# A hybrid encoder layer on one core: fewer idle matmuls, a recurrence prepared a step later, and a reordered final norm

## The chip, the core and the metric

The kernel runs on one NeuronCore of a Trainium2 chip. Its engines work side by side, each through a queue of its own: TensorE (PE, matrix products, with its weight loads shown apart as PEld), VectorE (DVE), ScalarE (ACT), GpSimd (POOL), and SyncE (SP), which issues most transfers between the chip's main memory and the core's own memory. The metric is the time of one execution on the device in microseconds (us); the median of three runs is 2256.15 us.

## The reference

One encoder layer over two groups of 256 tokens with 2048 features; both groups use the same weights.

```python
def encoder_layer(h, ...):
    xn = rmsnorm(h, norm_mix_w)
    proj = xn @ w_in                                  # 2048 x 7200
    y_na = neighbourhood_attention(q, k, v, na_rpb)   # 8 heads of 128, on a grid 4 x 64
    y_dn = gated_deltanet_bidir(qkv, z, b, a, ...)    # 8 heads of 128, chunks of 64 tokens
    h = h + concatenate([y_na, y_dn]) @ w_out
    hn = rmsnorm(h, norm_ffn_w)
    return h + (silu(hn @ w_gate) * (hn @ w_up)) @ w_down     # 5632 wide
# afterwards: rmsnorm(h, final_norm_w)
```

The gated delta rule passes a state of 128 x 128 per head from chunk to chunk, forward over the tokens and, in a second copy, backward. In each chunk:

```python
v_new = u_i - w_i @ S
o = (q_i * exp(g_i)) @ S + qk_i @ v_new
S = S * exp(g_last) + (k_i * exp(g_last - g_i)).T @ v_new
```

The output of both directions is added, normalised per head, and gated by silu(z). The final norm multiplies each token by 1 / sqrt(mean of squares + eps) and each feature by its weight.

## The kernel before

**Layout.** Features lie on the 128 partitions, the 512 tokens of both groups along the row: a tile of 128 features x 512 tokens is one of 16 row tiles of h. Large products are made in fp32r with operands split into a high and a low part, three matmuls for each (`mm3`: high x high, high x low, low x high). `load_w` loads a weight block through SP and splits it: `w_hi` on ACT (L138), `w_lo` on DVE (L139). Half of a column tile (`half_gemm`) is 8 x 3 matmuls of 128 x 512.

**Start.** While the first weights and rows of x arrive, `WARM` = 36 matmuls of 128 x 256 on a tile of ones in bf16 keep TensorE running; their result is not used. `load_first` splits weights (L274, L275) and `split_x` splits x (`xhi` on ACT, L256, `xlo` on DVE, L257). The first two column tiles then go row tile by row tile: six matmuls for each.

**The order of the work.** All matmuls and transposes are pinned to the order in which the program writes them. Small work is woven into the large products by generators: after every six large matmuls `half_gemm` calls `pump`, which advances the first generator of the queue `chains` and then the first of `side`. One such call is a step; `yield from pause(n)` lets n steps pass. The other engines' queues are ordered by the planner of the framework, by the order in the program and its own cost estimates; `tc.high_priority` moves the weight splits ahead.

**The recurrence.** Heads go in pairs. For a pair, two column tiles give v (each evacuated by `evac`, tile `ev_xi`, convolved on DVE in `conv_silu`, tile `cacc`, and passed through silu on ACT into `dvT`, L361), then `start_waiting` appends `prepare` of both heads, joined by `together`, to `side`, and `recur_pair` to `chains`. `prepare(h)` waits until the pair before has run its recurrence, fetches `uq` (POOL) and `kq` (SP) where that hasn't been done, pauses `2 + h % 2` steps, and transposes vT and kq in four blocks each (L90); ACT copies the first into `dvn` (L778), DVE scales the second into `kd` (L783). `recur_pair` waits for both heads, pauses `CORE_START` = 2 steps and runs four chunk steps. In each, `ps_s<-S,kq`, then DVE's `r` (L814), then `ps_s<-r,uq` and ACT's `n` (L828), then `ps_s<-n,kd` and the new state `S` (L848), with fixed pauses of 3, 2 and 2 steps between. At its end `finish_pair` goes to `side`: ACT takes eight squares (`yo`, L876), one step later DVE makes the factors (`ssq`, Newton steps L162 to L167, L882) and scales the outputs `os` (L887), and after `FIN_GAP` = 5 more steps TensorE transposes them (`ps_s<-ident,os`). The two z tiles of the pair follow the v tiles; after the last pair, the products of w_out with the attention half cover what is left of the recurrence.

**The end.** `finish` adds the last segment of w_down to h for one half of the tokens after the other (`hT`, L1318), squares each row tile (`f_sq`, L1355), scales it by the norm weight (L1356) and sums the squares (L1358). The last row tile's squares aren't summed there: `final_norm` sums `acc` and the last `sq` over the partitions with matmuls against ones, into one PSUM column for each 128 tokens, takes root and reciprocal (`sd`), scales the identity by each (`dgs`, L1334, two instructions on DVE), and one matmul of ones with `dgs` spreads the factors over all partitions. DVE multiplies h in six pieces (L1343), and SP stores each piece. The first half's norm runs within the second half's products; the second half's is the end of the program. PSUM tiles of the small work come from `sm_tile` (three banks).

Of the kernel before, what the change touches and what calls it, by code (L numbers as in the profile page):

```python
# [12 lines left out]
AF = mybir.ActivationFunctionType  # L13
ALU = mybir.AluOpType
# [4 lines left out]
P = 128  # L19
# [40 lines left out]
OPEN_AT = 0  # L60
HALF, BAND = 32, 40

WARM = 36

ROW_FACTORS = 24
DECAY_HEAD = 3
# [3 lines left out]
def r32(ap):  # L70
    return ap.bitcast(F32)
# [3 lines left out]
def hybrid_encoder(ctx: ExitStack, tc: tile.TileContext, xT, w_in, w_ba, w_out, w_gate,  # L75
# [3 lines left out]
    act = nc.scalar.activation  # L79
    tt = nc.vector.tensor_tensor  # L80
    ts = nc.vector.tensor_scalar
# [4 lines left out]
    def mm(*a, **k):  # L86
        pin(nc.tensor.matmul(*a, **k))  # L87

    def transpose(*a):
        pin(nc.tensor.transpose(*a))  # L90
# [12 lines left out]
    ones = cons.tile([P, P], F32, name="ones")  # L103
# [3 lines left out]
    ident = cons.tile([P, P], F32, name="ident")  # L107
# [92 lines left out]
    def pause(n):  # L200
        for _ in range(n):
            yield
# [11 lines left out]
    def col_tile(src, xs):  # L214
        ps = pg.tile([P, T], F32, tag="g", name="ps_g")
        half_gemm(ps, src[0], xs[:8], True, False)
        half_gemm(ps, src[1], xs[8:], False, True)
        return ps
# [20 lines left out]
    def sm_tile():  # L239
        return psm.tile([P, T], F32, tag="s", name="ps_s")  # L240
# [19 lines left out]
    ps = sm_tile()  # L260
    idle = ones.bitcast(BF16)
    for _ in range(WARM):
        mm(ps[:, :2 * P], idle[:, :P], idle, start=True, stop=True)
# [349 lines left out]
    for h in range(H):  # L613
        kq = wk.tile([P, 2, T], F32, tag="kq", bufs=2, name="kq")
        ps = (ps_k0, ps_k1)[h] if h < 2 else col_tile(w_in[2 * h], xs)
        conv_silu(ps, 8 + h, kq[:, 0])
        ps = (ps_q0, ps_q1)[h] if h < 2 else col_tile(w_in[2 * h + 1], xs)
        conv_silu(ps, h, kq[:, 1])
        sq = na.tile([P, T], F32, tag="qT", name="q_sq")
# [27 lines left out]
    ps = sm_tile()  # L647
# [66 lines left out]
    for h in range(H):  # L714
        ps = col_tile(w_in[16 + 3 * h], xs)
# [4 lines left out]
        ps = col_tile(w_in[16 + 3 * h + 1], xs)  # L720
# [4 lines left out]
        ps = col_tile(w_in[16 + 3 * h + 2], xs)  # L725
# [26 lines left out]
    def fetch(h):  # L752

        uq = state["UQ"][2 * (h % 2):2 * (h % 2) + 2]
        kq = wk.tile([P, 2, T], F32, tag="kq", bufs=2, name="kq2")
        nc.sync.dma_start(kq, s_kq[h])
        for b in range(NB):
            for hf in range(2):
                nc.gpsimd.dma_start(
                    uq[b][half[hf], :, :, hf * C:hf * C + C].rearrange("s i w c -> s (i w) c"),  # L760
                    s_uq[h * NB + b, hf].rearrange("s i w c -> s (i w) c"))
        fetched[h] = uq, kq

    def prepare(h, vT):

        dr = state["dr"]
        while h > 1 and not {h - 2, h - 2 ^ 1} <= traced:
            yield
        if h not in fetched:
            fetch(h)  # L770
        uq, kq = fetched[h]
        yield from pause(2 + h % 2)
        pv, pk = sm_tile(), sm_tile()
        for t, u in ((pv, vT), (pk, kq[:, 0])):
            for i in range(4):
                transpose(t[:, i * P:i * P + P], u[:, i * P:i * P + P], ident)
        vn = na.tile([P, NB, 2, P], F32, tag=("vT", "s1")[h % 2], name="dvn")
        nc.scalar.copy(vn, pv.rearrange("p (b q d) -> p b q d", b=NB, q=2))  # L778
        kd = dr.tile([P, 3, NB, P], F32, tag="kd", bufs=2, name="kd")
        pk4 = pk.rearrange("p (b q d) -> p b q d", b=NB, q=2)  # L780
        for st in range(3):
            pp = 0 if st in (0, 3) else 1
            tt(kd[:, st], pk4[:, :, pp],  # L783
               scs[:, st, h * NB:h * NB + NB, None].broadcast_to([P, NB, P]), ALU.mult)
        prepared[h] = (uq, kq, vn, kd)
        yield
# [121 lines left out]
    def start_waiting():  # L908
        open_recurrence()
        while state and waiting:  # L910
            h, vT = waiting.pop(0)
            side.append(together(prepare(h, vT[0]), prepare(h + 1, vT[1])))
            chains.append(recur_pair(h))

    late = []
    for h in range(0, H, 2):
        vT = []
        for i in range(2):
# [9 lines left out]
            ps = pg.tile([P, T], F32, tag="g", name="ps_g")  # L928
# [10 lines left out]
        for i in range(h, h + 2):  # L939
            ps = col_tile(w_in[40 + 2 * i + 1], xs)  # L940
# [24 lines left out]
    for i in pairs:  # L965
        ps = pg.tile([P, T], F32, tag="g", name="ps_g")
# [9 lines left out]
    for i in pairs[:2]:  # L976
        ps = pg.tile([P, T], F32, tag="g", name="ps_g")
# [20 lines left out]
    acc = gA.tile([P, T], F32, tag="acc", name="ssq_acc2")  # L998
    A11, S3, S1, A12, S2, S4, A22 = range(7)
    for n, i in enumerate(pairs):  # L1000
# [3 lines left out]
        else:  # L1004
            hk = st.tile([P, T], F32, tag="hk", bufs=2, name="hk")
            nc.sync.dma_start(hk, s_h1[i])
            ps = pg.tile([P, T], F32, tag="g", name="ps_g")
# [19 lines left out]
        sq = acc if n == 0 else st.tile([P, T], F32, tag="sq", name="h_sq")  # L1027
# [163 lines left out]
    for p in range(NPAIR):  # L1191
# [8 lines left out]
        if p // 2 == FIRST_SEG:  # L1200
            k = p % 2 * 2
# [31 lines left out]
    def ring(shape, nm):  # L1233
        return fq.tile([P] + shape, F32, tag="ra", bufs=5, name=nm)
# [86 lines left out]
    def final_norm(b, acc, sq):  # L1321
        t0, t1 = b * L, b * L + L
        yield from pause(2)
        ps = sm_tile()
        for i in range(2):
            for part in (acc, sq):
                mm(ps[:, i:i + 1], part[:, i * P:i * P + P], ones[:, :1], start=(part is acc),
                   stop=(part is sq), skip_group_check=True)
        sd = cons.tile([P, 2], F32, tag="sd", bufs=2, name="sd3")
        act(out=sd, in_=ps[:, :2], func=AF.Sqrt, scale=1.0 / D, bias=epsc)  # L1330
        nc.vector.reciprocal(sd, sd)
        dgs = qp.tile([P, 2, P], F32, tag="dgs", name="dgs")
        for i in range(2):
            ts(dgs[:, i], ident, sd[:, i:i + 1], None, ALU.mult)  # L1334
        yield from pause(3 if b == 0 else 0)
        rs = sm_tile()[:, :L]
        mm(rs, ones, dgs.rearrange("p i t -> p (i t)"), start=True, stop=True)
        if b:
            out = r32(state["new_sA"]()).rearrange("p a k t -> p (a k t)") \
                .rearrange("p (k t) -> p k t", t=L)  # L1340
        for k, n in ((0, 2), (2, 2), (4, 4), (8, 4), (12, 2), (14, 2)):
            yo = out[:, k:k + n] if b else ring([n, L], "yo")
            tt(yo, hT[k // 8][:, k % 8:k % 8 + n, t0:t1],  # L1343
               rs[:, None, :].broadcast_to([P, n, L]), ALU.mult)
            nc.sync.dma_start(y[b, k // 4, :, k % 4:k % 4 + n], yo)
            yield

    def finish(s, aseg, b, keep):

        t0, t1 = b * L, b * L + L  # L1350
        acc = qp.tile([P, L], F32, tag="acc", bufs=2, name="ssq_acc3")
        for n in down_half(s, aseg, t0, t1, keep):
            hk = hrow(n)[:, t0:t1]
            sq = acc if n == 0 else qp.tile([P, L], F32, tag="fsq", bufs=2, name="f_sq")
            act(out=sq, in_=hk, func=AF.Square)  # L1355
            act(out=hk, in_=hk, func=AF.Copy, scale=nwl[:, n:n + 1])  # L1356
            if 0 < n < 15:
                tt(acc, acc, sq, ALU.add)  # L1358
            pump()
        chains.append(final_norm(b, acc, sq))  # L1360
# [98 lines left out]
```

## Time and profile before

| | |
|---|---|
| median of 3 runs | 2256.15 us (2255.93 to 2256.17) |
| profiled execution | 2255.7 us, its span 2253.9 us |
| busy: PE, PEld, DVE, ACT, POOL | 2239.9, 1919.7, 1776.7, 1031.2, 236.6 us |
| share of the chain that ended last | PE 95%, DVE 2%, DMA 1%, ACT 1%, issue 1% |
| transfers | 381.20 MB, mean 169 GB/s |

In timeline rows the first column is the start in us from the span's start, the second the time from the first to the last of the row's instructions, then engine, line, operation, out<-in, shape and count; the brackets give the idle time of the engine before them and what ended it. Rows of waits give who waited, for whom, and us in total, times, longest. Rows of windows give, for a stretch, its length and the busy us (and count) of PE, PEld, DVE, ACT and POOL, then TensorE's granted clock, the mean busy share of the 16 DMA engines, and GB/s. The ends of matmuls are modelled: two that follow each other overlap in the trace, and only their starts tell how fast they go.

### The profile page before, as it was taken

Reading aid. Unit: us, or ns where it says so; the run is one execution under the profiler, and the core shown is the slowest. Engines: PE = TensorE matmul, PEld = TensorE weight load, DVE = VectorE, ACT = ScalarE, POOL = GpSimd, SP = SyncE. Lnnn points to the kernel's source line nnn. Section 1 sums busy time; section 2 is a strip of 40 time slices with the busy share of each in tenths; the row PEclk is TensorE's granted clock in tenths of the full one; section 3 lists DMA queues with packets and bytes.
Section 4 is the critical chain, followed back from the end, with each engine's and each line's share of the span. In section 5 each row is a group of like instructions: output and inputs, shape, how many; then the busy total and the mean of one; then the engine's idle time right before and its main releaser. Section 6 shows DMA issues by size and latency. Waiting matters only on the chain.

```text
span 2253.9 us, 32472 instructions
## 1 busy us (share of the span) xinstructions
PE 2239.9 (99%) x12314; PEld 1919.7 (85%) x12314; DVE 1776.7 (79%) x2728; ACT 1031.2 (46%) x1548; POOL 236.6 (10%) x370
## 2 busy tenths in 40 slices
PE   9999999999999999999999999999999999999998
PEld 7888888888888888888888888888888888888887
DVE  7954799964566537888888888888888798898966
ACT  6664433333443325554444444444444464444435
POOL 1321000010000011101101111101100001001010
PEclk9999999999999999999999999999999999999999
DMA  5344322363333555777777777777777467667682
GB/s 210 130 140 148 108 97 94 106 147 122 105 104 103 192 177 187 210 203 202 203 207 199 194 199 203 215 204 202 201 195 195 147 177 212 175 179 205 175 206 84
DMA packets 112540, 381.20 MB, mean 169 GB/s; under 512 B 14048, under 2 KB 14384, under 8 KB 112128
## 3 DMA queue, kind: packets, MB, share of 16 engines
q1 hardware_dynamic: 77552, 266.25, 34.9%
q0 software_dynamic: 33680, 110.78, 23.7%
q8 instruction: 97, 1.59, 0.3%
q10 hardware_dynamic: 1152, 2.10, 0.3%
q14 instruction: 59, 0.48, 0.1%
HBM read 343.66 MB, written 35.41 MB: 168 GB/s over the span
## 4 chain that ended last, share of the span: by engine, by line
PE 95%; DVE 2%; DMA 1%; ACT 1%; issue 1%; DVEq 0%; ACTq 0%
PE ps_g L87 36%; PE ps_c L87 14%; PE ps_d L87 14%; PE ps_a L87 14%; PE ps_s L87 8%; PE ps_b L87 7%; DMA w_raw<-in_w_in_dram 1%; PE ps_s L90 1%; PE ps_o L87 1%; DVE w_lo L139 1%; DVE cacc L357 0%; PE ps_e L87 0%; ACT yo L876 0%; ACT w_hi L138 0%; DVE aA L1343 0%
## 5 line engine op out<-in xcount | busy, mean ns | idle before, releaser
L87 PE MATMUL ps_g<-xhi,w_hi 128*128 128x512 f32 x880 | 351.4, 399 | 0.0
L87 PE MATMUL ps_g<-xhi,w_lo 128*128 128x512 f32 x880 | 343.4, 390 | 0.0
L87 PE MATMUL ps_g<-xlo,w_hi 128*128 128x512 f32 x880 | 342.8, 390 | 0.0
L138 ACT ACTIVATE w_hi<-w_raw 128x1024 fp32r<-128x1024 f32 x164 | 173.3, 1058 | 270.5 <-PE ps_g L87 209.6
L138 ACT ACTIVATE w_hi<-b 128x1024 fp32r<-128x1024 f32 (+1 forms) x180 | 185.8, 1032 | 238.0 <-issue 119.4
L139 DVE TENSOR_TENSOR w_lo<-w_raw,w_hi 128x1024 fp32r<-128x1024 f32 x164 | 200.3, 1221 | 100.3 <-ACT w_hi L138 100.0
L138 ACT ACTIVATE w_hi<-w_first 128x1024 fp32r<-128x1024 f32 (+1 forms) x180 | 185.5, 1030 | 180.9 <-PE ps_c L87 90.8
L139 DVE TENSOR_TENSOR w_lo<-w_first,w_hi 128x1024 fp32r<-128x1024 f32 (+1 forms) x180 | 213.8, 1188 | 60.2 <-ACT w_hi L138 56.7
L139 DVE TENSOR_TENSOR w_lo<-b,w_hi 128x1024 fp32r<-128x1024 f32 (+1 forms) x180 | 213.0, 1184 | 7.2 <-ACT w_hi L138 6.7
L87 PEld LDWEIGHTS ps_g<-xhi,w_lo 128*128 128x128 f32 x880 | 165.2, 188 | 36.1 <-DVE w_lo L139 0.4
L87 PEld LDWEIGHTS ps_g<-xhi,w_hi 128*128 128x128 f32 x880 | 165.4, 188 | 35.6 <-issue 2.9
L87 PEld LDWEIGHTS ps_g<-xlo,w_hi 128*128 128x128 f32 x880 | 165.5, 188 | 32.4
L87 PE MATMUL ps_d<-xc,w_hi 128*128 128x512 f32 x704 | 175.1, 391 | 0.0
L87 PE MATMUL ps_c<-xc,w_hi 128*128 128x512 f32 x704 | 175.1, 391 | 0.0
L87 PE MATMUL ps_a<-xc,w_hi 128*128 128x512 f32 x696 | 173.1, 391 | 0.0
L87 PEld LDWEIGHTS ps_c<-xc,w_hi 128*128 128x128 f32 x704 | 129.4, 188 | 25.0
L87 PEld LDWEIGHTS ps_d<-xc,w_hi 128*128 128x128 f32 x704 | 129.3, 188 | 25.0
L87 PEld LDWEIGHTS ps_a<-xc,w_hi 128*128 128x128 f32 x696 | 127.9, 188 | 24.8
L138 ACT ACTIVATE w_hi<-w_second 128x1024 fp32r<-128x1024 f32 (+1 forms) x60 | 62.0, 1033 | 93.2 <-DVE ga L1153 50.3
L87 PE MATMUL ps_d<-xc,w_lo 128*128 128x256 f32 x704 | 98.5, 283 | 0.0
L87 PE MATMUL ps_c<-xc,w_lo 128*128 128x256 f32 x704 | 98.5, 283 | 0.0
L87 PE MATMUL ps_a<-xc,w_lo 128*128 128x256 f32 x696 | 97.4, 283 | 0.0
(389 smaller groups left out, 4211.7 us busy)
## 6 DMA issues: line engine op xcount, KB each, us to landing
w_raw<-in_w_in_dram SPq DMA_DIRECT2D x108, 512.0 KB, 3.3
b<-in_w_gate_dram SPq DMA_DIRECT2D x66, 512.0 KB, 4.2
b<-in_w_up_dram SPq DMA_DIRECT2D x66, 512.0 KB, 4.6
b<-in_w_group_dram SPq DMA_DIRECT2D x48, 448.0 KB, 4.2
w_raw<-in_w_out_dram SPq DMA_DIRECT2D x32, 512.0 KB, 3.5
w_raw<-in_w_down_dram SPq DMA_DIRECT2D x24, 512.0 KB, 3.6
w_second<-in_w_gate_dram SPq DMA_DIRECT2D x22, 512.0 KB, 7.0
w_first<-in_w_gate_dram SPq DMA_DIRECT2D x22, 512.0 KB, 4.3
```

What stands on the lines that cost most here:

```text
L87: pin(nc.tensor.matmul(*a, **k))
L90: pin(nc.tensor.transpose(*a))
L138: act(out=hi, in_=src, func=AF.Copy)
L139: tt(lo, src, r32(hi), ALU.subtract)
```

## The change

There are five edits. `WARM` goes from 36 to 30. `prepare` pauses `3 + h % 2` steps rather than `2 + h % 2`. In `final_norm`, both matmuls on `acc` come ahead of both on the last squares, and only the first of the four has the start flag; the scaling of the identity for the second 128 tokens goes to ACT; and the first two output pieces have one and three row tiles rather than two and two.

```diff
--- before.py
+++ after.py
@@ -60,7 +60,7 @@
 OPEN_AT = 0
 HALF, BAND = 32, 40
 
-WARM = 36
+WARM = 30
 
 ROW_FACTORS = 24
 DECAY_HEAD = 3
@@ -769,7 +769,7 @@
         if h not in fetched:
             fetch(h)
         uq, kq = fetched[h]
-        yield from pause(2 + h % 2)
+        yield from pause(3 + h % 2)
         pv, pk = sm_tile(), sm_tile()
         for t, u in ((pv, vT), (pk, kq[:, 0])):
             for i in range(4):
@@ -1322,23 +1322,23 @@
         t0, t1 = b * L, b * L + L
         yield from pause(2)
         ps = sm_tile()
-        for i in range(2):
-            for part in (acc, sq):
-                mm(ps[:, i:i + 1], part[:, i * P:i * P + P], ones[:, :1], start=(part is acc),
+        for part in (acc, sq):
+            for i in range(2):
+                mm(ps[:, i:i + 1], part[:, i * P:i * P + P], ones[:, :1], start=(part is acc and i == 0),
                    stop=(part is sq), skip_group_check=True)
         sd = cons.tile([P, 2], F32, tag="sd", bufs=2, name="sd3")
         act(out=sd, in_=ps[:, :2], func=AF.Sqrt, scale=1.0 / D, bias=epsc)
         nc.vector.reciprocal(sd, sd)
         dgs = qp.tile([P, 2, P], F32, tag="dgs", name="dgs")
-        for i in range(2):
-            ts(dgs[:, i], ident, sd[:, i:i + 1], None, ALU.mult)
+        act(out=dgs[:, 1], in_=ident, func=AF.Copy, scale=sd[:, 1:2])
+        ts(dgs[:, 0], ident, sd[:, 0:1], None, ALU.mult)
         yield from pause(3 if b == 0 else 0)
         rs = sm_tile()[:, :L]
         mm(rs, ones, dgs.rearrange("p i t -> p (i t)"), start=True, stop=True)
         if b:
             out = r32(state["new_sA"]()).rearrange("p a k t -> p (a k t)") \
                 .rearrange("p (k t) -> p k t", t=L)
-        for k, n in ((0, 2), (2, 2), (4, 4), (8, 4), (12, 2), (14, 2)):
+        for k, n in ((0, 1), (1, 3), (4, 4), (8, 4), (12, 2), (14, 2)):
             yo = out[:, k:k + n] if b else ring([n, L], "yo")
             tt(yo, hT[k // 8][:, k % 8:k % 8 + n, t0:t1],
                rs[:, None, :].broadcast_to([P, n, L]), ALU.mult)
```

## The prediction

> **What bounds the kernel now.** I read the page first (engines, chain, groups), then TensorE's waits, then the timeline at the three places that the diff touches: the start, the recurrence, the end.
>
> ```profile
> span 2253.9 us, 32472 instructions
> PE 2239.9 (99%) x12314; PEld 1919.7 (85%) x12314; DVE 1776.7 (79%) x2728; ACT 1031.2 (46%) x1548; POOL 236.6 (10%) x370
> ```
>
> TensorE is busy 2239.9 of 2253.9 us: all that a change outside the matmuls can win is in the other 14 us, and in gaps between matmuls that the modelled ends hide. The profiled execution took 2255.7 us (1.8 around its span); the median of the runs is 2256.15, so 0.45 is added at the end. TensorE's own waits (what waited <- for what: us, times, longest):
>
> ```profile
> PE ps_s L90 <- ACT dvT L361: 1.5, 3, 0.6
> ...
> PE ps_s L87 <- DVE epsc L110: 1.1, 1, 1.1
> ...
> PE ps_s L90 <- DVE os L887: 0.3, 1, 0.3
> ```
>
> The first row is `prepare`, which the diff moves by one step; the last is `finish_pair`, which follows from it. TensorE's order is the order written in the program, so a time won at any place reaches the end, unless a later operand was ready only just in time. I found no such place after the start: these waits are nearly all.
>
> **Six fewer idle matmuls.** The start in the timeline:
>
> ```profile
> 1.25 2.13 PE L87 MATMUL ps_s<-ones 128*128 128x256 bf16 x9
> 2.74 1.49 PE L87 MATMUL ps_s<-ones 128*128 128x256 bf16 x6
> 6.76 1.15 PE L87 MATMUL ps_s<-ones 128*128 128x256 bf16 x9
> 7.42 0.49 PE L87 MATMUL ps_s<-ones 128*128 128x256 bf16 x3
> 7.67 0.48 PE L87 MATMUL ps_g<-xhi,w_hi 128*128 128x512 f32 x1
> ...
> 6.31 0.75 DVE L257 SCALAR_TENSOR_TENSOR xlo<-x_raw,nwm,xhi 128x512 fp32r<-128x512 f32 x1 [0.74 <-ACT xhi L256]
> ...
> 9.44 1.42 DVE L257 SCALAR_TENSOR_TENSOR xlo<-x_raw,nwm,xhi 128x512 fp32r<-128x512 f32 x2 [0.77 <-ACT xhi L256]
> ...
> 10.73 0.39 PE L87 MATMUL ps_g<-xlo,w_hi 128*128 128x512 f32 x1
> ...
> 2.00:3.00 1.00, 1.00 (x7) 0.69 (x6) 0.00 (x0) 0.22 (x2) 0.92 (x4) 1.00 0.53 122
> ```
>
> Nine idle matmuls take 2.13 us and six 1.49: one each (2.13 - 1.49)/3 = 0.213 us. Late, nine take 1.15 and three 0.49: 0.110 each. So the rate doubles at about 6.7 (the granted clock, 1.00 in the last row, doesn't show it), when some 27 of the 36 have run; the six that go are fast ones, 6 x 0.110 = 0.66 us, and the first real matmul could start at 7.0. Its operands are there: xhi released the xlo split at 6.31, which ends at 7.06, in time for the second matmul. Next to be late is xlo of the third row tile: the two splits from 9.44 are 0.71 each, so the first is done at 10.15 to 10.2, and the matmul that reads it starts at 10.73, a margin of 0.54. The start thus gains at least 0.54 less some 0.05 of signalling: **0.49**, bounds 0 (a transfer that comes later in another execution takes the margin) and 0.66.
>
> The Trainium skill (TensorE: Matmul & The Clock Gate, part 1) says that the array runs at half clock for its first 3.4 us or so of activity, whatever the number of matmuls, and that the window runs freely. By it the step were at 1.06 + 3.4 = 4.5, the 36 would end near 6.7 and the 30 near 6.0, xhi would come last, and this part would gain some 0.35. The trace disagrees: the step is at 6.7, 5.6 us in. By its other half the step may come later than the thirtieth matmul in some executions; then real matmuls do the warming that idle ones did, which costs nothing against before.
>
> **The recurrence prepared one step later.** A step is one `pump`, six matmuls. `prepare` transposes vT and kq of a pair's two heads in two successive steps; the second head's vT comes late. Without and with a wait (second pair):
>
> ```profile
> 86.28 10.89 PE ps_g L87 x48
> ...
> 591.44 0.39 PE L87 MATMUL ps_g<-xhi,w_lo 128*128 128x512 f32 x1
> 591.67 0.60 PE L90 MATMUL ps_s<-ident,dvT 128*128 128x128 f32 x4
> ...
> 592.46 0.47 PE L87 MATMUL ps_g<-xhi,w_hi 128*128 128x512 f32 x1
> ...
> 593.70 0.40 PE L87 MATMUL ps_g<-xhi,w_lo 128*128 128x512 f32 x1
> 594.67 0.85 PE L90 MATMUL ps_s<-ident,dvT 128*128 128x128 f32 x4 [0.58 <-ACT dvT L361]
> ...
> 595.72 0.48 PE L87 MATMUL ps_g<-xhi,w_hi 128*128 128x512 f32 x1
> ```
>
> A step is 6 x 10.89/48 = 1.36 us. From matmul to matmul the round takes 592.46 - 591.44 = 1.02 without and 595.72 - 593.70 = 2.02 with the wait: 1.00, though only 0.58 shows as idle, so 0.42 more each. Three waits of 1.5 in all cost 1.5 + 3 x 0.42 = **2.8 us**. One step (1.36) is more than the longest wait (1.00), so by itself the edit ends all three. The transfers, vn and kd of `prepare`, and the first core step, move with it: recurrence steps stay as far apart as they were, and the last pair ends long before the w_out products that cover it.
>
> What follows is in the queue `side`, which runs one generator at a time. Steps are counted by the 128x512 matmuls in the timeline, from the z tile of head 0 (its first is 12); between 587.76 and 591.67, steps 47 and 49, lie twelve. Pair 0 ends its recurrence at step 41, `finish_pair` transposes at 47, and only then `prepare` of the second pair runs (49, 50; its v tiles ended at 43). So the second pair is late by two steps, not one (51, 52); the third by three (81, 82 for 78, 79, since it waits for the second pair to be traced). The third now ends at 108, after the last v tile (107), so `prepare` of the fourth goes ahead of the third's `finish_pair`: 111, 112 for 113, 114, two steps earlier, yet free of the finishing work that held up its conv on DVE. The refill of uq (POOL) and kq (SP) starts when the earlier pair is done and has seven steps to its first use, where the third pair had six without a wait of TensorE.
>
> `finish_pair` is next to be late. Its squares (ACT), factor chain and scaling (DVE) end just before its transposes:
>
> ```profile
> 582.98 0.38 DVE L880 TENSOR_SCALAR ssq<-ssq 128x8 f32<-128x8 f32 x1 [2.81 <-ACT yo L876]
> ...
> 586.86 1.43 DVE L887 TENSOR_TENSOR os<-os,ssq 128x256 f32<-128x256 f32 x4
> 588.21 0.68 DVE L307 TENSOR_TENSOR ev_xi<-ps_g,rstd 128x512 f32<-128x512 f32 x1
> 589.14 1.22 DVE L139 TENSOR_TENSOR w_lo<-w_raw,w_hi 128x1024 fp32r<-128x1024 f32 x1
> ...
> 582.86 1.04 ACT L138 ACTIVATE w_hi<-w_raw 128x1024 fp32r<-128x1024 f32 x1
> ...
> 587.76 1.30 PE L90 MATMUL ps_s<-ident,os 128*128 128x128 f32 x8
> ...
> 667.58 1.03 PE L90 MATMUL ps_s<-ident,os 128*128 128x128 f32 x8
> ...
> 717.24 1.30 PE L90 MATMUL ps_s<-ident,os 128*128 128x128 f32 x8
> ...
> 787.15 1.30 PE L90 MATMUL ps_s<-ident,os 128*128 128x128 f32 x8 [0.29 <-DVE os L887]
> ```
>
> Eight take 1.03 where nothing is late and 1.30 where the scaling ends beside them. In pair 0 the eight squares now straddle the weight split that ACT makes after step 43 (1.04); the DVE split (1.22) then falls into DVE's wait rather than into the chain, so I count 0.5 more wait there, and 0.2 left at the second pair's vT, whose ev_xi stands behind this chain. The third pair's finish gets a `prepare` ahead of it as the second's had (1.03): 0.3 won. The fourth's I leave. So 2.8 - 0.5 - 0.2 + 0.3 = **2.4**. Bounds: below, 2.8 + 0.3 less a wait of 1.04 + 1.22 = 2.3 at pairs 0 and 3: -1.5; above, all finish waits gone too (three rounds of 1.30 - 1.03 and the idle 0.29): 2.8 + 1.1 = 3.9. I take the middle, since the queued order on DVE is the planner's and unknown.
>
> **The end.** The square sums change their order and a start flag, the two scalings split over DVE and ACT, the pieces their sizes:
>
> ```profile
> 2242.52 0.38 PE L87 MATMUL ps_s<-ones,f_sq 128*128 128x1 f32 x2 [0.59 <-ACT f_sq L1355]
> ...
> 2242.98 0.36 PE L87 MATMUL ps_s<-ones,f_sq 128*128 128x1 f32 x2
> 2243.38 0.26 ACT L1330 ACTIVATE sd<-ps_s,epsc 128x2 f32<-128x2 f32 x1 [0.38 <-PE ps_s L87]
> 2243.68 0.17 DVE L1331 RECIPROCAL sd<-sd 128x2 f32<-128x2 f32 x1 [1.66 <-ACT sd L1330]
> 2243.88 0.48 DVE L1334 TENSOR_SCALAR dgs<-ident,sd 128x128 f32<-128x128 f32 x2
> ...
> 2245.21 4.74 DVE L1343 TENSOR_TENSOR aA<-hT,ps_s 128x512 f32<-128x512 f32 x6 [0.85 <-PE ps_s L87]
> ...
> 779.49 0.40 ACT L876 ACTIVATE yo<-os,rqs 128x128 f32<-128x128 f32 x1
> ...
> 2248.00:2249.00 1.00, 0.00 (x0) 0.00 (x0) 1.00 (x2) 0.00 (x0) 0.00 (x0) 0.50 0.70 274
> ...
> 2250.00:2251.00 1.00, 0.00 (x0) 0.00 (x0) 0.00 (x0) 0.00 (x0) 0.00 (x0) 0.50 1.05 414
> ```
>
> Square sums first: behind the late f_sq now stand three pairs, 0.46/2 = 0.23 apart; then two. **0.23** won. Scalings on two engines: 0.48 on DVE against one ACT scaling; nearest row, 128x128 with a scale per partition, 0.40: **0.08** won, bounds -0.1 (signalling to a further engine) and 0.2. It waits for DVE's reciprocal; behind it in ACT's queue stands nothing at the end, and the next f_sq and hT scaling in the first half, where TensorE has a full row of matmuls before it needs them. First piece of one row: the pieces (1, 3) hold the rows of (2, 2), so the third piece, and all behind it, leave DVE at the same time; the DMA engines (share 0.70 in the slice where they wait for it, then 1.05) are busy from there on. A first piece earlier by half of a 0.68 piece fills no later gap: **0**, bounds 0 and 0.3. The same edits for the first half of the tokens lie under the matmuls of the second; uncovered they would be worth the same 0.3.
>
> **Sum**: 0.49 + 2.4 + 0.3 = 3.2. Span 2253.9 - 3.2 = 2250.7, execution 2252.5, median 2253.0.
>
> **Rivals.** *The waits only change place*: the finish chain, or ev_xi behind it on DVE, takes what dvT gave back. For it: ev_xi begins right behind os at 588.21. Against: the fourth pair escapes it. Gain 0.8: 2255.3.
>
> *Slower*: the two weight splits both land in the finish chain of pairs 0 and 3, which wait 2.3 more each. The transposes stand in TensorE's fixed order and all matmuls wait behind them. 0.49 + 2.8 + 0.3 - 4.6 = -1.0: 2257.2; it decides from 1.8 us per finish on. For it: DVE sat idle 2.81 us before the chain rather than doing ev_xi. The Trainium skill (TensorE: Matmul & The Clock Gate, part 1, engine queue depths) calls the DVE queue strictly in order, and this row agrees. Against: today's chain holds one of the splits at 0.3.
>
> *More*: finish waits go too and the start gives 0.66: 0.66 + 3.9 + 0.5 = 5.1, 2251.1. *The start doesn't pay*, its margin taken by a late transfer: 2253.5.
>
> **How the numbers follow.** Forecast 0.66 (own range 2251.8 to 2254.2), waits change place 0.12, start doesn't pay 0.08, more 0.08, slower 0.06. Range 2251.0 to 2255.4 leaves out the slower rival and edges of the others. 0.2% is 4.5 us, about what a measurement of this kernel can tell from no change: only "more" gets there, in part: faster 0.07; slower by that much needs three finish waits of the rival's size: 0.03; the same 0.90.
>
> **What would show it.** First real matmul near 7.0, and ps_g split margins near zero at the third row tile; no row dvT among TensorE's waits; prepare at steps 15, 16, 51, 52, 81, 82, 111, 112; sd some 0.23 after the first f_sq pair less than now. Wrong if the os row grows beyond 2 us, or if a new wait for r or S appears.

## The result, and the profile after

The changed kernel takes 2253.36 us (median; 2251.93 to 2254.94), the kernel before, measured beside it, 2256.27 (2254.84 to 2257.85): a ratio of 0.9986, 95% interval 0.998 to 0.9992, so 2.9 us less. The forecast was 2253.0. The profiled execution of after took 2253.6 us with a span of 2251.8; its counterpart of before had 2255.7 and 2253.9.

The page of after, its first lines, TensorE's share of the chain that ended last, and the group of matmuls that read w_lo:

```profile
span 2251.8 us, 32459 instructions
...
PE 2238.1 (99%) x12308; PEld 1918.6 (85%) x12308; DVE 1776.8 (79%) x2726; ACT 1031.3 (46%) x1550; POOL 236.6 (11%) x370
...
PE 91%; DVE 4%; DMA 2%; issue 1%; ACT 1%; POOL 0%; SPq 0%; DVEq 0%; ACTq 0%; POOLq 0%
...
L87 PE MATMUL ps_g<-xhi,w_lo 128*128 128x512 f32 x880 | 343.4, 390 | 0.8 <-DVE w_lo L139 0.8
```

The chain was 95% TensorE before and is 91% now: DVE and DMA have come into it. TensorE's waits of after say where (who waited <- for whom: us in total, times, longest):

```profile
PE ps_g L87 <- DVE w_lo L139: 0.8, 1, 0.8
PE ps_s L90 <- ACT dvn L778: 0.7, 2, 0.4
PE ps_g L87 <- DVE xlo L257: 0.6, 2, 0.3
```

The waits for dvT (1.5, three times) and for os are gone. New are a wait for w_lo, which the prediction did not have at all, two short ones for dvn, and two for xlo at the start.

**The start** of after, in the timeline:

```profile
6.39 0.51 PE L87 MATMUL ps_g<-xhi,w_hi 128*128 128x512 f32 x1
7.18 0.50 PE L87 MATMUL ps_g<-xlo,w_hi 128*128 128x512 f32 x1 [0.28 <-DVE xlo L257]
...
10.87 0.50 PE L87 MATMUL ps_g<-xlo,w_hi 128*128 128x512 f32 x1 [0.29 <-DVE xlo L257]
...
10.06 1.42 DVE L257 SCALAR_TENSOR_TENSOR xlo<-x_raw,nwm,xhi 128x512 fp32r<-128x512 f32 x2 [1.29 <-ACT xhi L256]
```

The first product matmul is 1.28 us earlier than before (7.67). The fourteenth, the first that reads xlo of the third row tile, is not: 10.87 against 10.73. The split that makes this xlo starts at 10.06 against 9.44.

**At 320 us** the w_lo wait; after, then before:

```profile
319.40 0.40 PE L87 MATMUL ps_g<-xlo,w_hi 128*128 128x512 f32 x1
320.64 0.50 PE L87 MATMUL ps_g<-xhi,w_lo 128*128 128x512 f32 x1 [0.84 <-DVE w_lo L139]
```

```profile
318.95 0.39 PE L87 MATMUL ps_g<-xlo,w_hi 128*128 128x512 f32 x1
319.36 0.50 PE L87 MATMUL ps_g<-xhi,w_lo 128*128 128x512 f32 x1
```

From one matmul to the next it is 1.24 us after and 0.41 before, so 0.83 more; two that follow each other without a wait start 0.23 apart, so before lost some 0.2 here as well. The chain that ended last runs into this matmul (start, us, what):

```profile
219.96 15.06 DMA kkq<-s_gram
...
243.71 2.20 DVE kkq L557
...
307.90 3.86 DVE kkq L604
...
319.45 1.15 DVE w_lo L139
320.64 3.93 PE ps_g L87 x16
```

It is the generator `lanes`: at 218 us GpSimd issues the reload of the Gram blocks of all heads into `kkq`, in four quarters (L506); ACT copies each to the other half of the partitions (L511); then DVE solves the triangular systems of all chunks side by side (L587, L589). In the windows of after DVE has no free time in this stretch:

```profile
292.00:302.00 10.00, 10.00 (x46) 8.30 (x46) 10.00 (x23) 2.15 (x3) 0.00 (x0) 1.00 0.38 131
302.00:312.00 10.00, 10.00 (x49) 8.43 (x48) 9.94 (x14) 0.57 (x1) 0.00 (x0) 1.00 0.17 54
```

The w_lo splits stand in the same queue among the solver's instructions. What ties them to the reload is ACT's queue: behind the last copy of `kkq` (235.05) ACT makes a w_hi, and DVE, idle for 7.47 us, waits for it. From 242 us on DVE is busy at least 9.1 of every 10 us.

```profile
238.69 1.04 ACT L138 ACTIVATE w_hi<-w_raw 128x1024 fp32r<-128x1024 f32 x1
...
239.77 1.23 DVE L139 TENSOR_TENSOR w_lo<-w_raw,w_hi 128x1024 fp32r<-128x1024 f32 x1 [7.47 <-ACT w_hi L138]
```

**The recurrence.** Transposes of the first finish and of the second pair's `prepare`, and what DVE and ACT do ahead of them, in after:

```profile
590.12 1.03 PE L90 MATMUL ps_s<-ident,os 128*128 128x128 f32 x8
595.09 0.60 PE L90 MATMUL ps_s<-ident,dvT 128*128 128x128 f32 x4
...
597.34 0.60 PE L90 MATMUL ps_s<-ident,dvT 128*128 128x128 f32 x4
598.35 0.66 PE L90 MATMUL ps_s<-ident,kq 128*128 128x128 f32 x4 [0.41 <-ACT dvn L778]
...
583.65 1.04 ACT L138 ACTIVATE w_hi<-w_raw 128x1024 fp32r<-128x1024 f32 x1
...
588.86 1.43 DVE L887 TENSOR_TENSOR os<-os,ssq 128x256 f32<-128x256 f32 x4
```

Large product matmuls are counted in the order of the program, those with w_in first, then those of w_out with the attention half. From the 1253rd (two behind the one that waits at 320 us) to the 2861st is 476.12 us before and 473.10 after, 3.0 us less. From there to the last matmul of w_down it is 1445.23 in both: in between nothing moved.

**The end** of after:

```profile
2240.79 0.61 PE L87 MATMUL ps_s<-ones,f_sq 128*128 128x1 f32 x4 [0.37 <-ACT f_sq L1355]
...
2241.43 0.26 ACT L1330 ACTIVATE sd<-ps_s,epsc 128x2 f32<-128x2 f32 x1 [0.15 <-PE ps_s L87]
2241.93 0.40 ACT L1333 ACTIVATE dgs<-ident,sd 128x128 f32<-128x128 f32 x1 [0.23 <-DVE sd L1331]
...
2243.11 4.75 DVE L1343 TENSOR_TENSOR aA<-hT,ps_s 128x256 f32<-128x256 f32 x6 [0.90 <-PE ps_s L87]
```

From the first matmul on f_sq to sd it was 2243.38 - 2242.52 = 0.86 before and is 0.64 now; from sd to the first piece, 2245.21 - 2243.38 = 1.83 before and 1.68 now; from the first piece to the end of the span 8.7 in both. So the sums gain 0.22, the scalings 0.15, the pieces nothing.

The profiled pair in one line: start +0.14, up to the 320 us place a further +1.14 (0.83 and smaller gaps around it), recurrence -3.02, end -0.36; sum -2.1, the difference of the spans.

### The profile page after: what moved, and what is told of

It is laid out like the page before. It is cut to its first block, busy times and chain, and to the rows that moved or that the text cites. A ratio compares the mean times of both kernels' runs of the same rounds, so it can differ in the third digit from the quotient of the medians.

```text
span 2251.8 us, 32459 instructions
## 1 busy us (share of the span) xinstructions
PE 2238.1 (99%) x12308; PEld 1918.6 (85%) x12308; DVE 1776.8 (79%) x2726; ACT 1031.3 (46%) x1550; POOL 236.6 (11%) x370
## 3 DMA queue, kind: packets, MB, share of 16 engines
q8 instruction: 97, 1.59, 0.3%
## 4 chain that ended last, share of the span: by engine, by line
PE 91%; DVE 4%; DMA 2%; issue 1%; ACT 1%; POOL 0%; SPq 0%; DVEq 0%; ACTq 0%; POOLq 0%
PE ps_g L87 32%; PE ps_c L87 14%; PE ps_d L87 14%; PE ps_a L87 14%; PE ps_b L87 7%; PE ps_s L87 7%; DMA w_raw<-in_w_in_dram 1%; DVE w_lo L139 1%; DVE prod L587 1%; DVE W L589 1%; PE ps_o L87 1%; DMA kkq<-s_gram 1%; PE ps_s L90 1%; PE ps_e L87 0%; ACT w_hi L138 0%
```

## The experiments

All times beside the kernel before are ratios to its runs on the same chip.

**Each part alone.** Before with 30 idle matmuls:

```diff
-WARM = 36
+WARM = 30
```

> Only the idle matmuls go from 36 to 30. If the start gains what the sum said, the time falls by about 0.5 us, and the product matmuls around 330 us of the span start 0.5 us earlier than in the kernel before. If the start is bound by the arrival of x and the stage near 320 us by the vector work of the lanes, the real matmuls begin earlier but the one on the third row tile's low part doesn't, and the time changes by less than 0.2 us.

Measured: 2256.48 us against 2256.32, ratio 1.0 (0.9991 to 1.0009). Fewer idle matmuls alone win nothing.

Before with the later step:

```diff
-        yield from pause(2 + h % 2)
+        yield from pause(3 + h % 2)
```

> Only the pause before the transposes is one step longer. If the recurrence carries the gain, the distance from the matmuls near 330 us to those near 800 us shrinks by 2.5 to 3.1 us and the time falls by as much; the three waits for dvT are gone. If the waits only change place, it shrinks by less than 1 us.

Measured: 2253.84, ratio 0.9988 (0.998 to 0.9997): -2.5 us. No wait for dvT or os is left, one for dvn is new (0.4). The stretch of the recurrence takes 472.55 us.

Before with the three edits of `final_norm` alone (the diff's last hunk):

> Only the three edits of the final norm. If the end is read rightly, the time from the end of the last squares to the end of the span shrinks by 0.3 to 0.4 us: 0.22 from the order of the sums, 0.1 to 0.15 from the scaling on two engines, nothing from the pieces. If the transfers bind the end, it doesn't shrink.

Measured: 2256.13, ratio 0.9999 (0.999 to 1.0007): -0.2. Against the expectation, the end of the profiled execution did not shrink. It is shown in the timeline, with one of its windows:

```profile
2242.53 0.61 PE L87 MATMUL ps_s<-ones,f_sq 128*128 128x1 f32 x4 [0.37 <-ACT f_sq L1355]
...
2244.12 1.22 PE L87 MATMUL ps_s<-dgs,ones 128*128 128x256 f32 x2 [0.98 <-ACT dgs L1333]
...
2245.37 4.74 DVE L1343 TENSOR_TENSOR aA<-hT,ps_s 128x256 f32<-128x256 f32 x6 [1.42 <-PE ps_s L87]
```

```profile
2244.00:2245.00 1.00, 0.88 (x2) 0.50 (x2) 0.00 (x0) 0.06 (x1) 0.00 (x0) 0.50 0.00 0
```

The two matmuls that spread the factors take 1.22 us here and 0.70 in after, as the next rows show: TensorE had fallen to half clock (0.50) before them, while after still has 1.00 at the same place.

```profile
2242.38 0.70 PE L87 MATMUL ps_s<-dgs,ones 128*128 128x256 f32 x2 [0.98 <-ACT dgs L1333]
```

```profile
2242.00:2243.00 1.00, 0.62 (x2) 0.30 (x2) 0.21 (x1) 0.33 (x1) 0.00 (x0) 1.00 0.00 0
```

From the first f_sq matmul to the first piece: 2.69 before, 2.32 after, 2.84 here. So the edits win 0.37 where the clock holds and lose 0.15 against the profiled before where it falls early; whether it does goes with the beat of the clock (last section), not with the edits.

After with 36 idle matmuls again, so everything but the start:

> The changed kernel with 36 idle matmuls again. If the start gains 0.5 us, this is 0.5 us slower than the changed kernel, so some 2.4 to 2.7 us faster than before. If the start gains nothing, it is as fast as the changed kernel, some 2.9 to 3.4 us faster than before.

Measured: 2253.45, ratio 0.9986 (0.9977 to 0.9994), the same as after. The three single parts add up to 0.2 - 2.5 - 0.2 = -2.5, all together give -2.9; the difference is within their intervals.

**Why the start is worth nothing.** The fourteenth product matmul against the landing of the third row tile of x, idle matmuls in brackets:

| | before (36) | after (30) | warm alone (30) | step alone (36) | norm alone (36) | all but warm (36) |
|---|---|---|---|---|---|---|
| x landed, us | 8.66 | 9.28 | 9.40 | 8.93 | 9.11 | 9.16 |
| first product matmul | 7.67 | 6.39 | 6.30 | 6.59 | 6.66 | 7.35 |
| fourteenth | 10.73 | 10.87 | 10.98 | 10.51 | 10.69 | 10.75 |
| behind the landing | 2.07 | 1.59 | 1.58 | 1.58 | 1.58 | 1.59 |

In five of the six this matmul comes 1.58 to 1.59 us behind the transfer, with 30 as with 36, wherever the first one was; so it does in all six of the further kernels below that have 30 or 36. That the time stays the same could not show it alone, since the intervals are wider than the 0.49 us in question. The profiled before is the exception: its x landed earliest, and its clock step was latest. In the starts of the idle matmuls the rate doubles at 6.7 us there, and between 4.5 and 6.1 in the others.

To see how far this goes, after with 12 idle matmuls:

```diff
-WARM = 30
+WARM = 12
```

> The changed kernel with 12 idle matmuls instead of 30. Theory of the gates: the matmul on the third row tile's xlo stays 1.6 us behind the landing of that tile and the matmul after the wait at 320 us stays 86.1 us behind the last copy of kkq, so the time stays at that of the changed kernel, within 0.3 us, although the first matmuls run longer on the half clock. Rival one (idle matmuls stand in the way): 18 fewer give a further 0.5 to 1 us. Rival two (they are needed for the clock): the clock rises later and the time is 0.5 to 1.5 us longer.

Measured: 2252.45, ratio 0.9983 (0.9974 to 0.9992), not told apart from after. Both distances that were expected to stay did not. The fourteenth matmul now comes 2.42 us behind its x, at 11.52, since the first products run on the half clock, until 10.51; the 320 us place passes at 320.42 (after 321.21) without a wait, because the last copy of kkq came at 233.88 (after 235.05).

**What holds the 320 us place.** The start of the last copy (L511), the matmul two ahead of the one that waits (the 1249th) and the one two behind it (the 1253rd); the last four kernels are told below:

| | last copy | 1249th | 1253rd | 1253rd less copy |
|---|---|---|---|---|
| before | 233.84 | 318.72 | 319.93 | 86.09 |
| after | 235.05 | 319.07 | 321.21 | 86.16 |
| warm alone | 234.67 | 319.11 | 320.80 | 86.13 |
| step alone | 235.12 | 319.09 | 321.23 | 86.11 |
| norm alone | 234.58 | 318.84 | 320.73 | 86.15 |
| all but warm | 235.03 | 318.97 | 321.11 | 86.08 |
| one step more | 234.74 | 318.74 | 320.89 | 86.15 |
| two queues, 30 | 234.09 | 318.79 | 320.61 | 86.52 |
| two queues, 36 | 234.24 | 318.97 | 320.77 | 86.53 |
| two queues, 12 | 234.74 | 320.08 | 321.24 | 86.50 |

The w_lo split itself, in before, in after and with 12 idle matmuls:

```profile
318.08 1.22 DVE L139 TENSOR_TENSOR w_lo<-w_raw,w_hi 128x1024 fp32r<-128x1024 f32 x1
...
319.37 1.22 DVE L139 TENSOR_TENSOR w_lo<-w_raw,w_hi 128x1024 fp32r<-128x1024 f32 x1
...
318.15 1.22 DVE L139 TENSOR_TENSOR w_lo<-w_raw,w_hi 128x1024 fp32r<-128x1024 f32 x1
```

It starts 84.24, 84.32 and 84.27 us behind the last copy of its kernel (233.84, 235.05, 233.88), whether TensorE waits for it, as in after, or comes too late to wait, as with 12. So DVE follows the copies, and not TensorE.

First an attempt to load earlier: heads 0 to 6 as soon as head 6 is stored, the last head's two lanes per group later.

```diff
+    def reload(n0, n1):
+        for k in range(4):
+            nc.gpsimd.dma_start(
+                kkq[16 * k + n0:16 * k + n1].rearrange("p s w c -> p s (w c)"),
+                s_gram[k, n0:n1].rearrange("n s w c -> n s (w c)"))
...
+        if h == H - 2:
+            reload(0, (H - 1) * NB)
...
-        for sl in quarters:
-            nc.gpsimd.dma_start(kkq[half[0], sl].rearrange("p s w c -> p s (w c)"), gram[:, sl])
+        reload((H - 1) * NB, H * NB)
```

> The changed kernel, with the reload of the Gram blocks into kkq split: the 14 lanes of each group that belong to heads 0 to 6 are loaded as soon as head 6's blocks are stored (about 195 us instead of 218 us), and only the two lanes of head 7 after it. Nothing else changes. Theory of the second gate (the six profiles put the matmul after the wait at 320 us at 86.1 us behind the last copy of kkq, which follows the landing of this reload): the copies end some 4 us earlier, the wait of 0.8 us for w_lo near 320 us goes, the stretch from the third row tile to matmul 1252 falls from 310.3 us to about 309.0 us, and the time comes out 1.0 to 1.3 us below the changed kernel, at about 2252.2 us. Rival (the 320 us place follows from something else, for example the scores and windows of VectorE, or TensorE itself): copies earlier, wait and time unchanged, 2253.4 us.

> The same early reload, with 36 idle matmuls instead of 30: with the gate at 320 us out of the way, the difference to the run before it is what six idle matmuls are worth by themselves. Theory that the third row tile's x is a gate of its own (its first matmul on xlo came 1.58 us after that landing in five of six profiles, with 30 or 36): no difference, within 0.2 us. Rival (the prediction's step: the start is worth 0.49 us and was only swallowed at 320 us): 0.3 to 0.6 us slower than with 30.

Measured: 2265.23, ratio 1.0041 (1.0029 to 1.0054), and with 36 idle matmuls 2264.82, ratio 1.004 (1.0027 to 1.0053): 8.6 and 8.2 us slower than before, where 2252.2 was expected of the first. The two differ by 0.4, within their intervals. GpSimd's timeline and TensorE's waits of the first:

```profile
194.27 2.05 POOL L369 DMA_DIRECT2D kkq<-s_gram  x4 [3.10 <-DMA s_gram<-gs]
...
219.21 2.42 POOL L393 DMA_DIRECT2D s_gram<-gs  x4 [12.77 <-ACT gs L391]
...
224.13 2.06 POOL L369 DMA_DIRECT2D kkq<-s_gram  x4 [1.92 <-DMA s_gram<-gs]
```

```profile
PE ps_s L90 <- ACT dvT L361: 3.8, 1, 3.8
```

The early part landed at 217.3. But the stores of head 7 went out at 219.2 instead of 212.6, and the last two lanes per group, an eighth of the bytes, took until 240.0, almost as long as the whole reload, in transfers of two partitions each. The planner moved the copies to 251.3 to 257.9 and with them the whole lane work, the stores of its result 19 us later (497.4 against 477.8), and the recurrence started late. It says nothing of the 320 us place; the early part was a poor way to ask.

Then the other direction: the first quarter loaded twice.

```diff
-        for sl in quarters:
+        for sl in quarters[:1] + quarters:
```

> The changed kernel with the first quarter of the reload of kkq done twice, which puts off the landing of the whole reload by one quarter's transfer (the four quarters landed 3.3 to 5.3 us apart) and leaves every other instruction in its place. Theory of the gate at 320 us: the last copy of kkq comes 3.5 to 5.5 us later, the matmul after the wait at 320 us again 86.1 us behind it, the wait for w_lo there grows from 0.8 to 4 to 6 us, and the time from 2253.4 to between 2256.5 and 2259 us. Rival (the equal distance of 86.1 us is only both hanging on TensorE's own progress): later copies, but no longer wait at 320 us and a time within 0.5 us of 2253.4 us.

Measured: 2257.98 (2254.77 to 2260.44), 4.6 above after. The time lies in the range that was expected, but not for the reason given: the last copy came 9.8 us later (244.82), the 1253rd matmul only 0.37 later, with the wait up from 0.8 to 1.8; the rest of the loss lies behind it:

```profile
PE ps_g L87 <- DVE w_lo L139: 2.3, 2, 1.8
PE ps_s L90 <- ACT dvn L778: 1.3, 2, 0.9
...
PE ps_s L90 <- ACT dvT L361: 0.4, 1, 0.4
```

The edit did not leave the rest in place: the planner put one more w_lo split ahead of the solver on DVE, and the multiplication with W (L604), which in after starts at 307.90 ahead of two w_lo splits, starts at 315.82 behind the first. So 86.1 us is no constant of the reload; it holds for one order of DVE's queue.

Then the same reload over two queues:

```diff
-        for sl in quarters:
-            nc.gpsimd.dma_start(kkq[half[0], sl].rearrange("p s w c -> p s (w c)"), gram[:, sl])
+        for q, sl in enumerate(quarters):
+            (nc.gpsimd, nc.sync)[q % 2].dma_start(
+                kkq[half[0], sl].rearrange("p s w c -> p s (w c)"), gram[:, sl])
```

> The changed kernel with quarters 1 and 3 of the same reload issued by SyncE instead of GpSimd, so that two queues carry it; same blocks, same order of the copies. Theory of the gate: the last copy comes 2 us or more earlier, the wait for w_lo at 320 us goes, and the time is 0.8 to 1.3 us below the changed kernel, at 2252.1 to 2252.6 us. Rival one (no gate there): 2253.4 us. Rival two (SyncE waits for the stores of the Gram blocks and the weight tiles behind it come late): a new wait of TensorE or ScalarE for w_raw around 220 to 230 us and 2254 us or more.

Measured: 2252.74 (2252.58 to 2253.53), ratio 0.9985 (0.9976 to 0.9994). The last copy is 0.96 earlier, less than the 2 us hoped for, the 1253rd matmul 0.60 earlier, and a wait of 0.6 is left. The distance grew to 86.5 since ACT has one more exponential of the attention (L680 in after) ahead of the w_hi that DVE waits for: it starts 4.05 us behind the last copy (238.14), in after 3.64.

```profile
PE ps_g L87 <- DVE w_lo L139: 0.6, 1, 0.6
```

The median is 0.6 below after's, but the intervals overlap, so no version here is shown to beat the changed kernel. At the end 0.38 us are lost: from the landing of the last output piece to the end of the span 1.34 us instead of 0.97.

> The same with 36 idle matmuls instead of 30: with the place at 320 us out of the way, what the six idle matmuls are worth. If the third row tile's x is a gate of its own, the same as the run before it within 0.3 us; if the start's step of the prediction (0.49 us) only lacked a free way, 0.3 to 0.7 us slower.

> The same with 12 idle matmuls. With 12 and the old reload the first product matmuls ran longer on the half clock, the third row tile's first matmul came at 11.52 us instead of 10.87, and the time stayed (2252.45 us) because the reload landed early in the runs shown. With the place at 320 us out of the way the late start should now show: 0.4 to 0.9 us slower than with 30. Rival: 12 are enough, and it is the fastest of all, below 2252 us.

Measured: 2252.63 with 36 (ratio 0.9984, 0.9975 to 0.9993) and 2253.3 with 12 (0.9986, 0.9977 to 0.9995). With 36 it is 0.1 below 30, as expected; with 12 it is 0.6 above, within the 0.4 to 0.9 expected, but the intervals of all three overlap. The place at 320 us wasn't out of the way in any of them, so they don't give the price of the start without it. They do bear on what holds the place. With 12, TensorE arrives 1.29 us later than with 30 (320.08 against 318.79), yet the 1253rd stays 86.50 us behind the last copy (86.52 and 86.53 in the other two). That TensorE's own progress sets the distance, the rival, falls with this and with the w_lo rows above.

**One step more.** After with pauses of 4 and 5:

```diff
-        yield from pause(3 + h % 2)
+        yield from pause(4 + h % 2)
```

> The changed kernel with the recurrence's steps prepared one step later still (4 and 5 instead of 3 and 4). Theory: the waits for dvT (5.1 us before, 3 us of them in the stretch that decides) are gone already with one step, and what is left there is 0.7 us of waits for dvn; a further step can win at most that, so 2252.7 to 2253.7 us, no wait for dvT. Rival: the step moves finishing work and transposes past one more product tile, and each move costs or gives as the first one did: 1 us or more either way.

Measured: 2256.31, ratio 0.9998 (0.9989 to 1.0007): the whole gain is gone. The expectation missed; its rival, 1 us or more either way, came out. TensorE's waits, its timeline and DVE's at the first finish, and the window behind it:

```profile
PE ps_s L90 <- DVE os L887: 2.5, 1, 2.5
```

```profile
590.40 0.39 PE L87 MATMUL ps_g<-xhi,w_lo 128*128 128x512 f32 x1
593.29 1.54 PE L90 MATMUL ps_s<-ident,os 128*128 128x128 f32 x8 [2.50 <-DVE os L887]
...
595.48 0.63 PE L87 MATMUL ps_g<-xhi,w_lo 128*128 128x512 f32 x1
595.90 0.63 PE L87 MATMUL ps_g<-xhi,w_hi 128*128 128x512 f32 x1
...
588.32 0.75 DVE L357 SCALAR_TENSOR_TENSOR cacc<-ev_xi,cw,cacc 128x508 f32<-128x508 f32 x1
...
592.38 1.43 DVE L887 TENSOR_TENSOR os<-os,ssq 128x256 f32<-128x256 f32 x4
```

```profile
595.00:598.00 3.00, 3.00 (x9) 2.32 (x8) 1.51 (x3) 0.52 (x1) 0.00 (x0) 0.56 0.00 0
```

In after the factor chain and the scaling of os run at 586.2 to 590.2 and ev_xi with the convolution comes behind them. One step later the convolution's four instructions of 0.75 us and a w_lo split of 1.23 fall among the factor chain; the scaling starts at 592.38 instead of 588.86, and TensorE waits 2.5 us. That idle time brings the clock down: the next eight product matmuls stand 0.43 apart instead of 0.23, 8 x 0.2 = 1.6 us more. 2.5 + 1.6 less the dvn waits saved (0.7) is 3.4; the recurrence takes 476.45 us instead of 473.10, 3.35 more. Of this kernel too one execution was profiled: two of its eleven runs took 2254.3 and 2254.5, the others 2255.8 to 2257.1, so the clock may not have fallen in every one.

## Why the prediction was right, and where it was not

**The time** (2253.0 against 2253.36) and the side are right, but one of the three terms is wrong and two are too small. That the number came out so near is luck in part: 0.49 too much at the start stands against some 0.8 too little in the recurrence.

**The recurrence, 2.4**: right in mechanism, small by some 0.8. Four kernels with the step and the old reload (after, step alone, all but warm, 12 idle) take 473.10, 472.55, 472.90 and 472.56 us for the stretch, three without it 476.12, 476.36 and 475.32: 3.15 on the mean. The waits for dvT end, as said, and the longest was shorter than the step. What was taken off was not due: 0.5 for the finish of pair 0, where ACT's split does straddle the squares at 583.65 as predicted, but os is scaled in time and the eight transposes take 1.03 instead of 1.30; the os wait of the last finish goes too. Not foreseen were the two waits of 0.3 to 0.4 for dvn, which shorten what is won. The order by steps came out, counted by the product matmuls as in the prediction: `prepare` at steps 15, 16, 51, 52, 81, 82, 111 and 112, behind the first pair's finish (590.12, 595.09), and for the fourth pair ahead of the third's (717.56, 733.36 in the timeline of after).

**The start, 0.49**: the step that failed. "The first real matmul could start" earlier was right (6.39 instead of 7.67, and not the 7.0 forecast, since the clock rose at 5.1 rather than 6.7), and the next operand to be late was indeed xlo of the third row tile. But the margin of 0.54 was read from one execution, in which x landed earlier than in any other and the clock rose later. In the other profiles with 30 or 36 there is no margin: the matmul follows the transfer at 1.58 to 1.59 us. The times agree but are too coarse to show it (+0.16, interval -2.0 to +2.0 us, for this edit alone; -0.1 between after and all but warm). The rival "the start doesn't pay", by a late transfer, is what happened, in five of the first six profiles. The rise that the prediction took from the one trace, 5.6 us in, was late by chance as well: in three of the six it came 3.5 to 3.6 us in, about where the rule quoted there puts it.

**"I found no such place after the start"** was wrong too. At 320 us TensorE's order runs into w_lo, held up by the solver on DVE. The waits of before don't show it, since in that execution the reload had landed early and only some 0.2 was lost. The page of before does not show it; a look at DVE's windows, full from 282 to 322 us, would have been a reason to doubt.

**The end, 0.3**: 0.22 and 0.15 and 0 against 0.23, 0.08 and 0, where the clock holds; where it falls before the spreading matmuls, the gain is lost.

**The rivals.** The waits did not just change place, and os did not grow, at this step. With one step more they do: a finish waits 2.5 us, as the slower rival said of two of them, though for the convolution and one split rather than for two splits, and the clock's 1.6 behind it is in neither rival.

**The sum.** 3.15 + 0.37 would be 3.5; the medians say 2.9. How much of the rest is the place at 320 us, which took 0.8 us more from the profiled after than from the profiled before, and how much the clock at the end, isn't settled: profiles show single executions. Nor is it settled why 12 idle matmuls cost nothing in the time although the fourteenth matmul is 0.65 later; the reload landed early there, and one profile doesn't tell chance from effect.

## What to carry to other kernels

Where the start waits for a transfer, read its margin from several executions: it moved by 0.7 us in the first six profiles (third row tile of x, 8.66 to 9.40), more than the 0.66 that the edit could win. A pause in a fixed order has a narrow best place: one step won 3 us and the next lost them, since each step decides which other work stands in front in the queues of DVE and ACT. When no wait shows in one trace, look for an engine that is full ahead of an operand; a reload's landing 85 us earlier can be what decides.

## What the runs showed of the hardware

**The clock's rise and fall keep a beat.** In four of the first six profiles TensorE was at full clock for 2239.14 us, in the others for 2235.73 and 2242.56 us: 656, 655 and 657 times 3.413. The beat's phase is a matter of the execution; with it change how many idle matmuls run slow (13 to 28 of 30 or 36) and whether the last two matmuls take 0.70 or 1.22 us. The Trainium skill (TensorE: Matmul & The Clock Gate, part 1) states a free-running window of 3413 ns: the trace agrees. The rise came 3.5 to 5.7 us after the first idle matmul in these six, and 2.6 to 5.8 in all twelve kernels with 30 or 36; with 12 it came after 9.5 and 10.5. These figures bound what raises the clock: of the interval of 3.41 us that ended at the rise, TensorE had been at work for 2.64 us in the earliest case (one step more), and in the latest (early reload, 36) an interval with 2.44 us of work had ended without a rise. In the first six the fall came 1.3 to 3.5 us after the end of the last square (f_sq), which itself ends 1.2 us after the start of the last product matmul.

**A wait of 2.5 us inside dense work cost 4.1 us**, for the half clock behind it. The Trainium skill (TensorE: Matmul & The Clock Gate, Why this matters for your kernels) warns of idle gaps over about 3 us; here a shorter one, with eight small transposes behind it, was enough. The clock was low from 594.21 to 597.62; the interval of the beat before it, from 590.80, began just as the idle time did, so the phase may have had a part in it.

**A transfer's time did not go by its bytes**: the four reload pieces of two partitions, 256 KB together, took from 224.1 to 240.0 us, the four of 64 partitions, 2 MB, from 218.4 to 235.0. In the trace each small piece is two packets of 32 KB, which take 2.1 to 3.5 us each, piece by piece one behind the other; each large piece is 64 packets of 8 KB. How much the weight stream beside them added wasn't separated.
